# Loading the next eight expert tiles' gates in three parts, in a hybrid attention and PEER kernel on one Trainium2 core

## The chip, the core and the metric

The kernel runs on one core of one Trainium2 chip. The core has a matrix engine (TensorE, PE in the profile, with its weight loads as PEld), a vector engine (VectorE, DVE), a scalar engine (ScalarE, ACT), a general engine (GpSimd, POOL) and an engine that here only starts transfers (SyncE, SP). Each works through its own queue in order and waits for the others by semaphores. Data come from device memory into the on-chip memory of 128 partitions through 16 DMA engines that all queues share. The metric is the device time of one execution in microseconds (us). A change is judged by the median of several executions against that of the kernel before.

## The reference, cut to what matters

One layer over 512 tokens of width 1024. First a gated part and an attention part are added to the input; then comes the part that this change touches, a product-key mixture of 16384 single-row experts (PEER):

```python
def block(xb):                     # tokens in blocks
    q = (xb @ w_query).reshape(PEER_TOKEN_BLOCK, PEER_HEADS, 2, PEER_HALF)
    sc = jnp.einsum('thpd,hpkd->thpk', q, sub_keys)
    s_top, i_top = lax.top_k(sc, PEER_TOPK)
    cand = s_top[:, :, 0, :, None] + s_top[:, :, 1, None, :]
    ...
    best, pos = lax.top_k(cand, PEER_TOPK)
    eidx = jnp.take_along_axis(cand_idx, pos, axis=-1)
    g = jax.nn.softmax(best, axis=-1)
    u = jnp.take(expert_u, eidx, axis=0)
    h = jax.nn.gelu(jnp.einsum('thkd,td->thk', u, xb))
    vv = jnp.take(expert_v, eidx, axis=0)
    return jnp.einsum('thk,thkd->td', (g * h).astype(xb.dtype), vv)
```

Each token picks 8 x 16 experts, weighs them by a softmax, and sums the rows of `expert_v` with the gate times the gelu of a dot product with the row of `expert_u`.

## The kernel before, in words

The 512 tokens are four tiles of 128. One of them, token tile 0, is computed by gathering: for each of its 128 chosen experts per token a row of `expert_u` and a row of `expert_v` is fetched by an indirect transfer from GpSimd (L863 and L874, 512 KB each), and VectorE forms the dot product (L865) and the weighted sum (L876). The other three, 384 tokens, are computed densely: all 16384 experts are multiplied, as 128 expert tiles of 128, and a gate matrix with mostly zeros selects. For 64 of these tokens the first product is spared too, so that the first product has 320 columns (NDU) and the second 384 (NDT).

A weight tile of 512 KB comes through SP into `raw` (L122, three buffers), ScalarE rounds it into `hi` (L124, five buffers), and VectorE, in some places GpSimd, takes the rest into `lo` (L125, five buffers). Products are made of three matmuls each, hi by hi, lo by hi and hi by lo (L140 to L142 for the first product, L932, L933 and L936 for the second).

Before the dense loop the gates of all tiles are made with one-hot matrices (L751) and stored by ScalarE's queue (L757) in `gd`, a tensor in device memory with one block for each eight expert tiles (GB = 8): 128 partitions of 24 groups (NG) of 16 tokens, each group with 8 tiles times 16 tokens in float32. That is 12 KB per partition and 1536 KB per block; there are 16 blocks.

The dense loop (L942) has 64 chunks of two expert tiles (BC = 2). In chunk c, `second_product` takes the two tiles of `expert_v` (`rows_of_v`, L760), multiplies the activations of the chunk by the gates (L910, which reads groups 0 to 19 of the block's tile `gc`), rounds them into `wh` (L911) and `wl` (L912), copies the gates of the 64 spared tokens into the rest of both (L921 and L922, groups 20 to 23), and runs 36 matmuls. Then, while chunks are left that have no first product yet (the first product runs 23 chunks ahead, AHEAD), the first products of chunk c + 23 follow, 48 matmuls with two tiles of `expert_u`. Both stand under a higher priority (PRIO). Behind them come, in chunks 0, 6, 12 and 18, the routing of a quarter of token tile 0 (`route_gathered`, whose scores `sc` are loaded at L847), and in each chunk a share of the gathers.

A block of gates serves four chunks. `gc` has two buffers. Block 0 is loaded by GpSimd in chunk 0, block 1 by SP in chunk 1, tied behind the last weight load so far (`tc.issue_after` puts an instruction behind another in its engine's queue), and block q + 1 by SP in chunk 4q, for q from 1 to 14, in the middle of `second_product`. Its buffer comes free when chunk 4q - 1 has read the block before last (L922).

The order on TensorE is as written (`tc.manual_schedule`). On the other engines a planner sets it when the kernel is built: it takes instructions by priority, which is program order but for the raised pieces, among those whose inputs and buffers are ready by its own estimate of times. The semaphores follow from the data. The names of the lines that matter are L122, L124 and L125 (weight tiles), L897 (the gate load), L910, L921 and L922 (its readers), L863, L865, L874 and L876 (the gathers) and L847 (the scores).

Of the kernel before, what the change touches and what calls it, by code (L numbers as in the profile page):

```python
# [8 lines left out]
F32 = mybir.dt.float32  # L9
# [10 lines left out]
P = 128  # L20
# [30 lines left out]
NB = 128  # L51
BC = 2
# [24 lines left out]
GB = 8  # L77
TC = 8
TG = 16
NG = NDT // TG  # L80
# [7 lines left out]
def hybrid_block(tc, x, ln1, w_in, gng, wsT, bsb, qkg, bias, w_out, ln2, wq, skT, uT, ud, vd, out):  # L88
    nc = tc.nc
    ctx = ExitStack()  # L90
    with ctx:
# [22 lines left out]
        loads = []  # L114
# [150 lines left out]
        with tc.tile_pool(name="preb", bufs=1) as preb:  # L265
# [124 lines left out]
            with tc.manual_schedule(engines={mybir.EngineType.PE}):  # L390
                for i in range(len(steps) + LAG + 3):
# [6 lines left out]
                    if 0 <= i - LAG < len(steps):  # L398
                        t, hs = steps[i - LAG]
                        for h in hs:  # L400
                            transposed(t, h)
                    if 0 <= i - LAG - 1 < len(steps):
                        t, hs = steps[i - LAG - 1]
# [288 lines left out]
        gd = dram.tile([NB // GB, P, NG, GB * TG], F32, name="gd")  # L692
# [67 lines left out]
        def rows_of_v(c):  # L760

            return [load_split(vd.rearrange("(a b) d -> a b d", b=NB)[:, c * BC + b, :]) for b in range(BC)]
# [16 lines left out]
        with tc.manual_schedule(engines=engines):  # L779
# [4 lines left out]
            for n in range(steps + LEAD):  # L784
                t, c = divmod(n, per)
# [50 lines left out]
        ep = ctx.enter_context(tc.tile_pool(name="ep", bufs=1))  # L836
# [55 lines left out]
        accs = [[acx[:, 0:512], acx[:, 512:]]] + [[pa() for _ in range(2)] for _ in range(ND - 1)]  # L892
        gcs = {}

        def load_gates(q, eng):
            gcs[q] = ep.tile([P, NG, GB, TG], F32, name="gc", tag="gc", bufs=2)
            eng.dma_start(gcs[q].rearrange("p n b t -> p (n b t)"), gd[q].rearrange("p n f -> p (n f)"))  # L897

        def second_product(c):
            w = weights.pop(c) if c in weights else rows_of_v(c)  # L900
            if c == 0:
                load_gates(0, nc.gpsimd)
            gc = gcs[c * BC // GB]
            act = acts.pop(c)
            wh = ep.tile([P, BC, NDT], F32R, name="wh", tag="wh", bufs=2)
            wl = ep.tile([P, BC, NDT], F32R, name="wl", tag="wl", bufs=2)
            for b in range(BC):
                bb = (c * BC + b) % GB
                av = act[:, b, :].rearrange("p (n t) -> p n t", t=TG)
                nc.vector.tensor_tensor(av, av, gc[:, 0:NDU // TG, bb, :], op=ALU.mult)  # L910
            nc.scalar.activation(wh[:, :, 0:NDU], act, AF.Copy)  # L911
            mark = nc.vector.tensor_tensor(wl[:, :, 0:NDU], act, wh[:, :, 0:NDU].bitcast(F32), op=ALU.subtract)  # L912
            if c == 1:
                with tc.issue_after(loads[-1]):
                    load_gates(1, nc.sync)
            elif c * BC % GB == 0 and 0 < c * BC < NB - GB:
                load_gates(c * BC // GB + 1, nc.sync)
            b0 = (c * BC) % GB
            gu = gc[:, NDU // TG:, b0:b0 + BC, :]
            hu, lu = (w_[:, :, NDU:].rearrange("p b (n t) -> p n b t", t=TG) for w_ in (wh, wl))  # L920
            nc.scalar.activation(hu, gu, AF.Copy)  # L921
            nc.vector.tensor_tensor(lu, gu, hu.bitcast(F32), op=ALU.subtract)  # L922
            order = [(b, t) for b in range(BC) for t in range(ND)]
            if c == NCHK - 1:
                order.sort(key=lambda bt: bt[1])
            for b, t in order:
                first = c == 0 and b == 0
                last = c == NCHK - 1 and b == BC - 1
                tok = slice(t * P, (t + 1) * P)
                for half in range(2):  # L930
                    ds_ = slice(half * 512, (half + 1) * 512)
                    nc.tensor.matmul(accs[t][half], wh[:, b, tok], w[b][0][:, ds_], start=first, stop=False)  # L932
                    nc.tensor.matmul(accs[t][half], wh[:, b, tok], w[b][1][:, ds_], start=False, stop=False)  # L933
                for half in range(2):
                    ds_ = slice(half * 512, (half + 1) * 512)
                    nc.tensor.matmul(accs[t][half], wl[:, b, tok], w[b][0][:, ds_], start=False, stop=last)  # L936
            return mark
# [3 lines left out]
        with tc.manual_schedule(engines={mybir.EngineType.PE}):  # L941
            for c in range(NCHK):  # L942
                with tc.high_priority(offset=PRIO):
                    mark = second_product(c)
                    if c + AHEAD < NCHK:
                        for _ in first_products((c + AHEAD) * BC, BC):
                            pass
                if c % ROUTE == 0 and c < PARTS * ROUTE:
                    route_gathered(c // ROUTE)
                passed = c + 1 + min(c + 1, NCHK - AHEAD)  # L950
                with tc.issue_after(mark.ins if hasattr(mark, "ins") else mark):
                    gather_some(min(total, total * max(0, passed - DELAY) // (weight - SLACK - DELAY))
                                - (total - len(gathers)))
            gather_some(len(gathers))
# [53 lines left out]
```

## Time and profile before

| what | value |
|---|---|
| median of 3 runs | 1493.92 us |
| lowest and highest | 1490.16 and 1494.91 us |
| the profiled execution's own time | 1489.67 us |
| its span, first to last instruction | 1487.9 us |
| mean granted TensorE clock | 0.984 |
| expert loop in it | from about 641 us to the end |
| gate loads | 1 by GpSimd at 630.5, 15 by SP from 648.5 to 1409.4 us |
| moved by DMA | 396.78 MB, 267 GB/s over the span |

The profile is of one execution; its times count from the first instruction. Busy time of an engine leaves out its waits. In a row of the timeline stand the start, the time, engine and line, the operation, the output and inputs by the program's names with their shapes, how many such instructions in a row, and in square brackets the time for which the engine stood idle before and what ended that wait. SPq and POOLq are the queues in which transfers are started. Matmuls are pipelined, so that each shows a longer time than its distance to the next. The granted clock is the share of full speed at which TensorE was allowed to run.

### The profile page before, as it was taken

The page shows a single profiled execution, that of the slowest core. Times are in us where ns is not written, and L with a number is a line of the kernel's source. Part 1 is how long each engine was busy: PE and PEld are TensorE (multiplying, and loading weights), DVE is VectorE, ACT ScalarE, POOL GpSimd, SP SyncE. Part 2 cuts the span into 40 slices and gives each one's busy share as a digit, 9 for nine tenths or more (in the row PEclk, how much of TensorE's full clock was granted, in tenths as well). Part 3 has the DMA queues.
Part 4 walks back from the last instruction along what each step waited for, and adds up shares of the span by engine and source line. Part 5 has one row for each costly group of instructions (what it writes and reads, how often), then busy time and mean ns, then how long its engine had stood idle before and what let it go on. Part 6 is the DMA issues. An engine that isn't in the chain of part 4 may idle for free.

```text
span 1487.9 us, 21702 instructions
## 1 busy us (share of the span) xinstructions
PE 1403.9 (94%) x7804; PEld 1235.9 (83%) x7804; DVE 1158.7 (78%) x2345; ACT 641.9 (43%) x1108; POOL 690.4 (46%) x470
## 2 busy tenths in 40 slices
PE   7999999998878888999989899999999999999998
PEld 6886678987777888888978799888999989888886
DVE  5437554699996968688988789898888888688883
ACT  5447534332335677743434333343343333333331
POOL 0000016687867966504435555464555554344530
PEclk9999999998998999999999999999999999999999
DMA  5352226576765976878878799999999999879992
GB/s 184 114 184 71 86 102 186 184 260 230 282 230 165 324 219 198 240 256 310 300 284 331 290 376 330 350 355 349 389 350 357 368 341 367 305 285 341 333 356 85
DMA packets 161420, 396.78 MB, mean 267 GB/s; under 512 B 12304, under 2 KB 74528, under 8 KB 159264
## 3 DMA queue, kind: packets, MB, share of 16 engines
q1 hardware_dynamic: 62992, 197.42, 37.4%
q0 software_dynamic: 47488, 171.50, 31.1%
q10 hardware_dynamic: 50832, 26.48, 6.3%
q8 instruction: 61, 1.00, 0.3%
q14 instruction: 47, 0.39, 0.1%
HBM read 363.86 MB, written 31.46 MB: 266 GB/s over the span
## 4 chain that ended last, share of the span: by engine, by line
PE 51%; DVE 19%; DMA 13%; issue 7%; POOL 5%; ACT 4%; ACTq 0%; SPq 0%; DVEq 0%; POOLq 0%
PE pu L140 6%; PE pu L142 6%; PE pu L141 6%; PE pa L932 5%; PE pa L933 5%; PE pa L936 5%; DMA row<-in_vd,eint 5%; DVE rowe L489 3%; PE px L933 3%; PE px L932 3%; PE px L936 3%; DMA row<-in_ud,eint 3%; PE pa L140 2%; PE pa L141 2%; PE pa L142 2%
## 5 line engine op out<-in xcount | busy, mean ns | idle before, releaser
L124 ACT ACTIVATE hi<-raw 128x1024 fp32r<-128x1024 f32 x300 | 317.3, 1058 | 511.0 <-DMA raw<-in_vd 185.2
L125 DVE TENSOR_TENSOR lo<-raw,hi 128x1024 fp32r<-128x1024 f32 x251 | 309.5, 1234 | 109.5 <-ACT hi L124 108.4
L874 POOL DMA_INDIRECT row<-in_vd,eint x128 | 196.9, 1538 | 196.8 <-DVE acc L876 165.2
L863 POOL DMA_INDIRECT row<-in_ud,eint x128 | 184.6, 1442 | 190.3 <-DVE row L865 149.1
L140 PE MATMUL pu<-xch,hi 128*128 128x320 f32 x816 | 257.7, 316 | 3.5 <-ACT act L546 2.9
L142 PE MATMUL pu<-xch,lo 128*128 128x320 f32 x816 | 252.6, 310 | 2.6 <-POOL lo L125 2.0
L141 PE MATMUL pu<-xcl,hi 128*128 128x320 f32 x816 | 252.5, 309 | 0.0
L932 PE MATMUL pa<-hi,wh 128*128 128x512 f32 x512 | 200.9, 392 | 0.0
L933 PE MATMUL pa<-lo,wh 128*128 128x512 f32 x512 | 200.5, 392 | 0.0
L876 DVE SCALAR_TENSOR_TENSOR acc<-row,hw,acc 128x1024 f32<-128x1024 f32 x128 | 165.1, 1290 | 40.4 <-DMA row<-in_vd,eint 40.1
L865 DVE SCALAR_TENSOR_TENSOR row<-row,xb 128x1024 f32<-128x1024 f32 x128 | 156.3, 1223 | 28.9 <-DMA row<-in_ud,eint 28.5
L140 PEld LDWEIGHTS pu<-xch,hi 128*128 128x128 f32 x816 | 154.7, 190 | 7.2 <-ACT act L546 5.0
L936 PE MATMUL pa<-hi,wl 128*128 128x512 f32 x512 | 158.1, 390 | 0.0
L142 PEld LDWEIGHTS pu<-xch,lo 128*128 128x128 f32 x816 | 154.3, 189 | 3.8 <-POOL lo L125 2.2
L141 PEld LDWEIGHTS pu<-xcl,hi 128*128 128x128 f32 x816 | 154.6, 189 | 1.5
L125 POOL TENSOR_TENSOR lo<-raw,hi 128x1024 fp32r<-128x1024 f32 x49 | 117.8, 2416 | 77.2 <-ACT hi L124 73.3
L751 PE MATMUL pa<-bm,am 128*128 128x128 f32 x768 | 99.0, 283 | 19.9 <-POOL bm L730 13.7
L751 PEld LDWEIGHTS pa<-bm,am 128*128 128x128 f32 x768 | 93.3, 196 | 25.1 <-POOL bm L730 22.6
L932 PEld LDWEIGHTS pa<-hi,wh 128*128 128x128 f32 x512 | 96.8, 189 | 20.6
L933 PEld LDWEIGHTS pa<-lo,wh 128*128 128x128 f32 x512 | 96.8, 189 | 20.5
L936 PEld LDWEIGHTS pa<-hi,wl 128*128 128x128 f32 x512 | 96.6, 189 | 20.6
L933 PE MATMUL px<-lo,wh 128*128 128x512 f32 x256 | 101.0, 395 | 7.2 <-DVE lo L125 7.2
(215 smaller groups left out, 2635.1 us busy)
## 6 DMA issues: line engine op xcount, KB each, us to landing
raw<-in_uT SPq DMA_DIRECT2D x128, 512.0 KB, 5.8
raw<-in_vd SPq DMA_DIRECT2D x128, 512.0 KB, 5.6
gd<-gst ACTq DMA_DIRECT2D x24, 1024.0 KB, 6.2
gc<-gd SPq DMA_DIRECT2D x15, 1536.0 KB, 9.7
raw<-in_w_in SPq DMA_DIRECT2D x20, 512.0 KB, 4.7
raw<-in_wq SPq DMA_DIRECT2D x16, 512.0 KB, 3.8
raw<-in_w_out SPq DMA_DIRECT2D x8, 512.0 KB, 4.2
bt<-in_bias SPq DMA_DIRECT2D x8, 256.0 KB, 7.4
```

The source lines that it names most:

```text
L124: nc.scalar.activation(hi, raw, AF.Copy)
L125: eng.tensor_tensor(lo, raw, hi.bitcast(F32), op=ALU.subtract)
L140: nc.tensor.matmul(ps, lh[0], rh[0], start=first, stop=False)
L141: nc.tensor.matmul(ps, lh[0], rh[1], start=False, stop=False)
L142: nc.tensor.matmul(ps, lh[1], rh[0], start=False, stop=last)
L751: nc.tensor.matmul(ps[:, i * P:(i + 1) * P], am[:, 4 * q + i, :], bm[:, 4 * q + i, :], start=True, stop=True)
L863: nc.gpsimd.indirect_dma_start(out=row, out_offset=None, in_=ud, in_offset=bass.IndirectOffsetOnAxis(ap=eint[:, j:j + 1], axis=0))
L874: nc.gpsimd.indirect_dma_start(out=row, out_offset=None, in_=vd, in_offset=bass.IndirectOffsetOnAxis(ap=eint[:, j:j + 1], axis=0))
L876: nc.vector.scalar_tensor_tensor(acc0, row, hw[:, j:j + 1], acc0, op0=ALU.mult, op1=ALU.add)
L932: nc.tensor.matmul(accs[t][half], wh[:, b, tok], w[b][0][:, ds_], start=first, stop=False)
L933: nc.tensor.matmul(accs[t][half], wh[:, b, tok], w[b][1][:, ds_], start=False, stop=False)
L936: nc.tensor.matmul(accs[t][half], wl[:, b, tok], w[b][0][:, ds_], start=False, stop=last)
```

## The change

Blocks 1 to 15 of the gates come in three transfers of 8 groups each (512 KB, 4 KB per partition), where they came in one of 24 groups. For block q + 1, part 0 stands in chunk 4q, part 1 in chunk 4q + 1 and part 2 in chunk 4q + 2, always behind L912. For block 1, parts 0 and 1 stand in chunk 1, tied behind the last weight load so far as the whole load was, and part 2 in chunk 2, without such a tie. All three parts write into the same `gc` tile, which is taken with part 0. Block 0 is still loaded whole by GpSimd. L910 and L921 read what they read before.

```diff
-        def load_gates(q, eng):
-            gcs[q] = ep.tile([P, NG, GB, TG], F32, name="gc", tag="gc", bufs=2)
-            eng.dma_start(gcs[q].rearrange("p n b t -> p (n b t)"), gd[q].rearrange("p n f -> p (n f)"))
+        def load_gates(q, eng, part=0, parts=1):
+
+            if part == 0:
+                gcs[q] = ep.tile([P, NG, GB, TG], F32, name="gc", tag="gc", bufs=2)
+            ns = slice(part * NG // parts, (part + 1) * NG // parts)
+            eng.dma_start(gcs[q][:, ns].rearrange("p n b t -> p (n b t)"),
+                          gd[q, :, ns].rearrange("p n f -> p (n f)"))
...
-            if c == 1:
-                with tc.issue_after(loads[-1]):
-                    load_gates(1, nc.sync)
-            elif c * BC % GB == 0 and 0 < c * BC < NB - GB:
-                load_gates(c * BC // GB + 1, nc.sync)
+            q, part = divmod(c, GB // BC)
+            parts = GB // BC - 1
+            if q + 1 < NB // GB:
+                if c == 0:
+                    pass
+                elif c == 1:
+                    with tc.issue_after(loads[-1]):
+                        load_gates(1, nc.sync, 0, parts)
+                        load_gates(1, nc.sync, 1, parts)
+                elif part < parts:
+                    load_gates(q + 1, nc.sync, part, parts)
```

## The prediction

> **What bounds the kernel now.** I read the page's header and engine shares first, then the stretches of the expert loop, then TensorE's waits in them.
>
> ```profile
> span 1487.9 us, 21702 instructions
> PE 1403.9 (94%) x7804; PEld 1235.9 (83%) x7804; DVE 1158.7 (78%) x2345; ACT 641.9 (43%) x1108; POOL 690.4 (46%) x470
> ```
>
> ```profile
> 670.00:870.00 200.00, 189.60 (x1014) 168.11 (x1014) 174.17 (x384) 76.44 (x112) 97.95 (x65) 0.98 0.84 310
> 870.00:1295.00 425.00, 424.45 (x2338) 383.26 (x2337) 364.85 (x465) 162.48 (x232) 221.53 (x151) 1.00 0.95 352
> 1295.00:1470.00 175.00, 175.00 (x773) 144.87 (x773) 137.36 (x178) 63.00 (x86) 67.03 (x43) 1.00 0.82 301
> ```
>
> The columns are stretch, length, then busy time and count of PE, PEld, DVE, ACT and POOL, then the granted clock, the DMA share and GB/s. From 870 to 1470 TensorE is busy for 599.45 of 600 us at a clock of 1.00: whatever the gates do there, nothing can be won. Only between 670 and 870 is there something to win: 200 - 189.60 = 10.4 us of idle PE, and a clock of 0.98, worth 0.02 x 200 = 4 us. So 14 us is the ceiling of any gain in the loop, 0.9% of the whole. The three longest holes, in the timeline of PE:
>
> ```profile
> 754.09 0.42 PE L140 MATMUL pu<-xch,hi 128*128 128x320 f32 x1 [1.68 <-ACT act L546]
> 768.65 0.59 PE L933 MATMUL px<-lo,wh 128*128 128x512 f32 x1 [2.88 <-DVE lo L125]
> 849.28 0.50 PE L933 MATMUL px<-lo,wh 128*128 128x512 f32 x1 [3.74 <-DVE lo L125]
> ```
>
> Two of them wait for VectorE's `lo`, the low half of a split weight tile. What VectorE and GpSimd did ahead of the one at 768.65:
>
> ```profile
> 755.91 1.68 POOL L874 DMA_INDIRECT row<-in_vd,eint  x1 [9.59 <-DVE acc L876]
> 765.77 1.28 DVE L876 SCALAR_TENSOR_TENSOR acc<-row,hw,acc 128x1024 f32<-128x1024 f32 x1 [4.38 <-DMA row<-in_vd,eint]
> 766.98 0.48 DVE L910 TENSOR_TENSOR act<-act,gc 128x320 f32<-128x320 f32 x1
> 767.38 1.22 DVE L125 TENSOR_TENSOR lo<-raw,hi 128x1024 fp32r<-128x1024 f32 x1
> ```
>
> ```profile
> 754.47 0.33 SPq L897 DMA_DIRECT2D gc<-gd  x1
> ```
>
> The `lo` that PE needs stands in VectorE's queue behind a gathered row that landed late (issued at 755.91, used at 765.77), while the gates' 1.5 MB, issued at 754.47, was in flight. The hole at 849.28 stands behind a gathered row too, but no gate load flies then: the last one before it was issued at 817.26, 30 us earlier.
>
> ```profile
> 817.26 0.52 SPq L897 DMA_DIRECT2D gc<-gd  x1
> 846.86 1.23 DVE L865 SCALAR_TENSOR_TENSOR row<-row,xb 128x1024 f32<-128x1024 f32 x1 [4.38 <-DMA row<-in_ud,eint]
> ```
>
> So the gate load is party to one hole out of the three.
>
> What the gate load costs its neighbours is read from the DMA issues of two short windows at full load, 1004.4 to 1010 with a gate load and 1022 to 1036 without one (the last number is the median from issue to landing):
>
> ```profile
> gc<-gd SPq DMA_DIRECT2D x1, 1536.0 KB, 11.0
> raw<-in_vd SPq DMA_DIRECT2D x1, 512.0 KB, 11.2
> row<-in_vd,eint POOLq DMA_INDIRECT x1, 11.0
> row<-in_ud,eint POOLq DMA_INDIRECT x1, 11.2
> ```
>
> ```profile
> raw<-in_vd SPq DMA_DIRECT2D x1, 512.0 KB, 6.1
> row<-in_vd,eint POOLq DMA_INDIRECT x3, 7.8
> row<-in_ud,eint POOLq DMA_INDIRECT x3, 7.5
> ```
>
> A weight tile queued behind the gates lands 11.2 - 6.1 = 5.1 us later, a gathered row 11.0 - 7.8 = 3.2 or 11.2 - 7.5 = 3.7 us later.
>
> **The change part by part.** It removes fifteen transfers of 1536 KB from SP's queue and puts 45 of 512 KB there. The bytes, the buffers and the readers are the same; tile 0 is still loaded whole by GpSimd.
>
> *Where the parts will stand.* In program order parts 1 and 2 come one and two chunks behind part 0, but only for tile 1 are parts 0 and 1 tied to a weight load. SP's order is the planner's, and the trace shows what the planner does with a load whose buffer is free:
>
> ```profile
> 658.36 0.33 SPq L122 DMA_DIRECT2D raw<-in_vd  x1
> 658.74 0.43 SPq L847 DMA_DIRECT2D sc<-s0d  x1
> ```
>
> ```profile
> 1015.80 3.30 DVE L910 TENSOR_TENSOR act<-act,gc 128x320 f32<-128x320 f32 x8
> ```
>
> The first `sc` load that SP issues is written behind chunk 6 of the loop. Chunks start near 641 and take some 15 us (425 us of full PE in 2338 matmuls, 84 to a chunk, is 15.3), so its place is near 733; it went out at 658.74. The L910 products show the same on VectorE: all eight of a gate tile, for four chunks, in one run as soon as it lands. One event, the last use of the buffer's earlier tile, frees the place of all three parts at once. So I expect the three issues back to back, or with a weight load between, not chunks apart: mostly the change will not do what its words say.
>
> *SP's time.*
>
> ```profile
> L897 SPq DMA_DIRECT2D gc<-gd x15: 326/327/1065, 648.5 to 1409.4; - x15
> L897 POOLq EVENT_SEMAPHORE  x8: 43/43/43, 619.8 to 630.0; - x8
> ```
>
> ```profile
> SPq L122 <- DVE lo L125: 523.6, 165, 9.6
> ```
>
> Thirty more issues of 0.33 us are 9.9 us of SP, which waits 523.6 us for weight buffers to come free: 0 on the path. Without that cover the load behind the parts goes out 0.66 us late. L910 reads groups 0 to 19 of 24, hence all three parts: two more waits per tile, 30 at the 43 ns of the nearest row, are 1.3 us of VectorE. VectorE is idle for 27.1 us between 641.3 and 870:
>
> ```profile
> 641.30:870.00 228.70, 201.57 (x482) 0.98 0.81 297
> ```
>
> So 0 again, and 1.3 us if the cover is gone.
>
> *The DMA engines' time.*
>
> ```profile
> DMA packets 161420, 396.78 MB, mean 267 GB/s; under 512 B 12304, under 2 KB 74528, under 8 KB 159264
> q1 hardware_dynamic: 62992, 197.42, 37.4%
> q0 software_dynamic: 47488, 171.50, 31.1%
> ```
>
> 161420 - 159264 = 2156 packets are of 8 KB or more, and 16 gate loads x 128 partitions are 2048: gates move in packets of 12 KB, where the change makes 4 KB ones. On q0 a packet takes 0.311 x 16 x 1487.9 / 47488 = 0.156 us for 3.6 KB, so by bytes 0.18 us for 4 KB and 0.53 us for 12 KB: the total stays. What may change is the turn of a gathered row beside the gates: 512 KB are 8 packets on each of 16 engines. If queues take turns by packets, a row sits out 8 x 0.53 = 4.2 us of gates, and 8 x 0.18 = 1.4 us after the change: 2.8 us sooner, the size of the 3.2 us measured above. If turns go by bytes, or the gates' neighbour is a weight tile in the same queue, nothing changes. Ends: 0 and -2.88 us, the hole at 768.65, plus its clock:
>
> ```profile
> 764.00:774.00 10.00, 7.12 (x24) 5.38 (x23) 8.23 (x14) 2.44 (x3) 0.95 (x1) 0.83 0.81 308
> ```
>
> 0.17 x 10 = 1.7 us, so -4.6 at most. I take half, -2.3 us, since both readings are open. The Trainium skill (DMA: Bandwidth & Descriptors, Queues, rings and completion order) says that each DMA engine serves the queue rows in turn, a packet at a time. By that rule the gather's 2.8 us are won, and the term would be near -4.6 instead of -2.3.
>
> *The loop's start.* Part 2 of tile 1 stands in chunk 2 and is tied to nothing, and its buffer is free from the start. Like the `sc` load it can go out as soon as the gates are stored, beside tile 0's load that PE waits for:
>
> ```profile
> 638.90 0.89 DVE L910 TENSOR_TENSOR act<-act,gc 128x320 f32<-128x320 f32 x2 [4.47 <-DMA gc<-gd]
> 630.00:640.00 10.00, 7.62 (x52) 7.36 (x51) 3.24 (x6) 2.36 (x5) 2.39 (x4) 1.00 0.98 394
> ```
>
> At a share of 0.98, 0.52 MB at 394 GB/s are 1.3 us. Ends: 0 (it hides behind weight tiles, which have time) and +1.3; I take +0.5, since it adds to another queue than tile 0's.
>
> *The other engines' order.* The planner orders the work again with other landing times. No row prices that. The ends are -14 us (all of 670 to 870 repaired) and +14 (its holes twice); I take 0.
>
> Sum: 1489.67 (the profiled execution: the span of 1487.9 and 1.77 around it) - 2.3 + 0.5 = 1487.9. The median of the three runs, 1493.92, lies 4.25 above the profiled one; on that footing the time is **1492 us**.
>
> **The rivals.** *Spread out after all, faster.* If a weight load becomes ready between the parts, each keeps one 512 KB part ahead of it and not three. Two thirds of the 5.1 us delay go, 3.4 us, and gathers lose their long neighbour. The hole at 768.65 goes whole with its clock, 4.6 us: 1489. For it: weight loads follow the gates within 2.3 us, so a little planner's time between the parts lets one in:
>
> ```profile
> 1004.48 0.33 SPq L897 DMA_DIRECT2D gc<-gd  x1
> 1006.81 0.33 SPq L122 DMA_DIRECT2D raw<-in_vd  x1
> ```
>
> Against it: one release for all three parts, and an SP that mostly waits.
>
> *VectorE waits for three landings, slower.* VectorE takes its queue in order, and L910 is put there early, by the planner's idea of when gates land. Where that idea is too early it already stands idle:
>
> ```profile
> 1350.95 2.10 DVE L910 TENSOR_TENSOR act<-act,gc 128x320 f32<-128x320 f32 x5 [3.47 <-DMA gc<-gd]
> ```
>
> After 1295 PE does not feel it. If the parts look quicker to the planner than one transfer, L910 moves forward everywhere, and `lo` stands behind it. Four gate loads go out on SP before 870, the first at 648.5 and the last at 817.3. VectorE's slack there is 27.1 us over 15 chunks, 1.8 us a chunk, so it decides once a wait exceeds 1.8: 3.47 - 1.8 = 1.7 us of PE for each of four tiles, 6.8, and clock in the ratio 4 to 10.4, 2.6: +9.4, so 1503. Against it: before 870 no wait of 3 us for gates delays PE now.
> The Trainium skill (DMA: Bandwidth & Descriptors, Anatomy of one DMA) gives each transfer, on GpSimd's path, some 2 us of fixed cost. Three in series would then cost 4 us more than one, an estimate, and this rival would hold; the rows above speak against a series: gates issued at 1004.48 landed 11.0 us later, the weight tile issued at 1006.81 11.2 us later, so 512 KB more came only 2.5 us behind, under full load.
>
> **How the numbers follow.** The forecast gets 0.45, with an own range of 1487 to 1497; spread out 0.28; the VectorE wait 0.27. A measurement of this kernel tells about 0.3% (4.5 us) from no change. Of the forecast 0.11 falls to faster, 0.30 to same, 0.04 to slower; of the spread, which lies just at the bound, 0.18 to faster and 0.10 to same; of the wait 0.07 to same and 0.20 to slower. Faster 0.29, same 0.47, slower 0.24. The range takes in the faster rival with 5 us of planner's luck below it and stops just short of the slower one: 1484 to 1502.
>
> **What would show it.** SP's timeline: three L897 issues within a microsecond or two (mine) or a chunk apart (the spread). Packets: near 165,260 in all (15 x 256 more), with some 240 of 8 KB or more. L897 at about 631 in SP's queue shows the start's term, and a PE gap before 641 its price. PE idle between 670 and 870 under 8 us says the gather term is real; over 16 us with L910 waiting for gates, the slower rival. I am wrong if PE gets holes behind 870, which would mean that the planner's new order costs more than any row here.

## The result, and the profile after

The changed kernel takes 1511.38 us (median of 4 runs, 1507.32 to 1520.42), where the kernel before took 1494.41 (4 runs). The ratio is 1.0116, with a 95% interval from 1.0076 to 1.0156: 17 us slower, where 1492 us, no change, was the forecast and 1502 the end of the range.

The profiled execution of the changed kernel (1507.32 us), its header and engine shares:

```profile
span 1505.5 us, 21751 instructions
PE 1413.2 (94%) x7804; PEld 1242.6 (83%) x7804; DVE 1164.1 (77%) x2345; ACT 642.6 (43%) x1108; POOL 688.9 (46%) x470
```

The first matmul of the second products, in the timeline of PE, after:

```profile
653.84 0.80 PE L942 MATMUL px<-hi,wh 128*128 128x512 f32 x1 [5.00 <-ACT wh L915]
```

and before:

```profile
641.28 0.50 PE L932 MATMUL px<-hi,wh 128*128 128x512 f32 x1 [3.66 <-ACT wh L911]
```

So of the 17.6 us between the two spans 12.6 lie ahead of the loop's start, in code that the change does not touch but for 5.00 - 3.66 = 1.3 us, and 5.0 behind it. These proportions are those of two single executions; the experiments below show others.

The stretches of the loop, after, moved back by 13 us so that they answer to those of before (the same columns):

```profile
683.00:883.00 200.00, 193.35 (x1045) 172.16 (x1044) 179.39 (x391) 77.74 (x113) 99.34 (x67) 0.99 0.86 317
883.00:1308.00 425.00, 419.68 (x2307) 377.67 (x2307) 359.11 (x460) 161.61 (x229) 222.36 (x150) 1.00 0.93 348
1308.00:1483.00 175.00, 171.40 (x750) 141.45 (x749) 137.20 (x177) 61.85 (x84) 64.29 (x43) 0.99 0.82 303
```

PE's idle time went from 10.4 to 6.7 us in the first stretch, from 0.6 to 5.3 in the second and from 0 to 3.6 in the third. In this execution what was won early was lost where PE had been full; the clean pair below has the loss without the early win.

SP's queue, after, at the loop's start and at the last block:

```profile
640.96 0.33 SPq L900 DMA_DIRECT2D gc<-gd  x1
641.34 0.42 SPq L122 DMA_DIRECT2D raw<-in_uT  x1
...
1423.67 0.86 SPq L900 DMA_DIRECT2D gc<-gd  x2
1427.11 0.33 SPq L122 DMA_DIRECT2D raw<-in_vd  x1
1427.49 0.65 SPq L900 DMA_DIRECT2D gc<-gd  x1
1430.17 14.27 SPq L122 DMA_DIRECT2D raw<-in_vd  x3
```

The parts do not go out a chunk apart, but two at once, one weight load, and the third. The untied part of block 1 stands ahead of weight loads at 640.96. The packets of the changed kernel:

```profile
DMA packets 165741, 396.79 MB, mean 264 GB/s; under 512 B 12784, under 2 KB 75008, under 8 KB 165504
```

165741 - 165504 = 237 packets of 8 KB or more are left of 2156. What the hole of 3.6 us in the third stretch waited for, from the timelines of ScalarE, VectorE and PE after, and the granted clock in the window behind it:

```profile
1435.57 1.06 ACT L124 ACTIVATE hi<-raw 128x1024 fp32r<-128x1024 f32 x1 [4.97 <-DMA raw<-in_vd]
```

```profile
1438.17 0.49 DVE L914 TENSOR_TENSOR act<-act,gc 128x320 f32<-128x320 f32 x1 [3.52 <-DMA gc<-gd]
1438.58 1.22 DVE L125 TENSOR_TENSOR lo<-raw,hi 128x1024 fp32r<-128x1024 f32 x1
1439.72 2.09 DVE L914 TENSOR_TENSOR act<-act,gc 128x320 f32<-128x320 f32 x5
1441.73 0.81 DVE L916 TENSOR_TENSOR wl<-act,wh 128x640 fp32r<-128x640 f32 x1
```

```profile
1442.60 1.22 PE L946 MATMUL px<-hi,wl 128*128 128x512 f32 x2 [3.60 <-DVE wl L916]
```

```profile
1442.60:1445.40 2.80, 2.80 (x7) 2.22 (x8) 2.80 (x5) 1.26 (x2) 0.00 (x0) 0.50 0.06 19
```

VectorE stands at the first product with the new gates; behind it in its queue are the `lo` and the `wl` of the work that PE needs now. The weight tile is late as well. After the hole PE runs 2.8 us at a clock of 0.50, which costs another 1.4 us. The same block before:

```profile
1409.43 0.42 SPq L897 DMA_DIRECT2D gc<-gd  x1
```

```profile
1419.16 2.10 DVE L910 TENSOR_TENSOR act<-act,gc 128x320 f32<-128x320 f32 x5 [3.02 <-DMA gc<-gd]
```

There VectorE had the gates 1419.16 - 1409.43 = 9.7 us after their issue, now 1438.17 - 1423.67 = 14.5 us.

### The profile page after: what moved, and what is told of

Same layout as the page of the kernel before. It is cut to its first block, busy times and chain, and to the rows that moved or that the text cites. A ratio compares the mean times of both kernels' runs of the same rounds, so it can differ in the third digit from the quotient of the medians.

```text
span 1505.5 us, 21751 instructions
## 1 busy us (share of the span) xinstructions
PE 1413.2 (94%) x7804; PEld 1242.6 (83%) x7804; DVE 1164.1 (77%) x2345; ACT 642.6 (43%) x1108; POOL 688.9 (46%) x470
## 2 busy tenths in 40 slices
DMA packets 165741, 396.79 MB, mean 264 GB/s; under 512 B 12784, under 2 KB 75008, under 8 KB 165504
## 4 chain that ended last, share of the span: by engine, by line
PE 58%; DVE 15%; DMA 10%; issue 7%; POOL 5%; ACT 4%; ACTq 0%; SPq 0%; DVEq 0%; POOLq 0%
PE pu L140 7%; PE pu L141 7%; PE pu L142 7%; PE pa L942 6%; PE pa L943 6%; PE pa L946 6%; DMA row<-in_vd,eint 4%; DVE rowe L489 3%; PE px L946 3%; PE px L942 3%; PE px L943 3%; PE pa L140 2%; PE pa L141 2%; PE pa L142 2%; DMA row<-in_ud,eint 2%
## 5 line engine op out<-in xcount | busy, mean ns | idle before, releaser
L124 ACT ACTIVATE hi<-raw 128x1024 fp32r<-128x1024 f32 x300 | 317.1, 1058 | 540.3 <-DMA raw<-in_vd 209.8
L125 DVE TENSOR_TENSOR lo<-raw,hi 128x1024 fp32r<-128x1024 f32 x251 | 309.1, 1232 | 104.4 <-ACT hi L124 103.2
L874 POOL DMA_INDIRECT row<-in_vd,eint x128 | 204.2, 1595 | 224.5 <-DVE acc L876 194.1
L863 POOL DMA_INDIRECT row<-in_ud,eint x128 | 175.8, 1374 | 167.4 <-DVE row L865 126.9
L876 DVE SCALAR_TENSOR_TENSOR acc<-row,hw,acc 128x1024 f32<-128x1024 f32 x128 | 165.8, 1295 | 42.3 <-DMA row<-in_vd,eint 41.9
L125 POOL TENSOR_TENSOR lo<-raw,hi 128x1024 fp32r<-128x1024 f32 x49 | 118.6, 2432 | 84.8 <-ACT hi L124 78.5
```

The lines of the kernel that those rows point to most:

```text
L124: nc.scalar.activation(hi, raw, AF.Copy)
L125: eng.tensor_tensor(lo, raw, hi.bitcast(F32), op=ALU.subtract)
L863: nc.gpsimd.indirect_dma_start(out=row, out_offset=None, in_=ud, in_offset=bass.IndirectOffsetOnAxis(ap=eint[:, j:j + 1], axis=0))
L874: nc.gpsimd.indirect_dma_start(out=row, out_offset=None, in_=vd, in_offset=bass.IndirectOffsetOnAxis(ap=eint[:, j:j + 1], axis=0))
L876: nc.vector.scalar_tensor_tensor(acc0, row, hw[:, j:j + 1], acc0, op0=ALU.mult, op1=ALU.add)
```

## The experiments

The recorded expectations weigh theories by name. TURNS is that gates in small packets lose their share of the DMA engines to the gathered rows, so that they, and the weight tiles behind them in SP's queue, land later. Its rivals were that the order or the number of the transfers costs, and that the loss is one of the time ahead of the loop. LAYOUT, a rival that comes in later, is that the order of the gates in device memory costs, not the size of their packets. All ratios are to the kernel before on the same chip, with 95% intervals.

**The two kernels again.** No edit.

> The changed kernel once more, unaltered. Three theories of the extra 17 us of the changed kernel (1511.38 against 1494.41 us). LOOP: the change costs 5 to 8 us itself, 1 to 2 at the loop's start (PE waits 5.0 us there against 3.7) and 4 to 6 in the loop (VectorE waits for three gate landings); then this run is 5 to 9 us above the kernel before. LUCK: the 11.2 us that were lost before 620 us, in instructions that are the same and in the same order, are chance: VectorE's L601 was caught behind GpSimd's L125 three times in eight where the kernel before was caught twice, at about 7 us each; then this run's profile has another number of caught L601 and the time before the loop moves by 7 us a piece. FIXED: the time before the loop is longer in every run of the changed kernel; then the profile again shows the loop's first second-product matmul near 654 us and the time is again 12 to 20 us above.

> The kernel before as its own rival, unaltered: a null. All theories: ratio 1.000. It shows how wide a ratio of two equal kernels comes out, and how many L601 are caught in another profile of the same program. LUCK expects a time before the loop that differs from the first profile's 641 us by 0 or about 7 or 14 us; FIXED expects 641 within 2 us.

The changed kernel: 1519.22 us, ratio 1.0107 [1.0081, 1.0133]. The kernel before: 1498.70 us, 0.9974 [0.9951, 0.9997]. The loss repeats. The second interval just leaves out 1 for two copies of one program, so differences near 0.3% are not told apart here. The kernel before also showed that its time ahead of the loop varies by itself; PE in its second profile:

```profile
651.54 0.80 PE L932 MATMUL px<-hi,wh 128*128 128x512 f32 x1 [3.67 <-ACT wh L911]
```

10.3 us later than in the first, with every instruction the same. The 11 us that the changed kernel's profile lost there need no change to explain them.

**Without the three parts' places.** Three parts, issued together where the whole load stood:

```diff
...
+            if c == 1:
+                with tc.issue_after(loads[-1]):
+                    for part in range(3):
+                        load_gates(1, nc.sync, part, 3)
+            elif c * BC % GB == 0 and 0 < c * BC < NB - GB:
+                for part in range(3):
+                    load_gates(c * BC // GB + 1, nc.sync, part, 3)
```

> The split alone: all three parts in the one place where the whole load stood (chunk 4q, and tied in chunk 1). If the split itself costs (three landings, L910 put earlier by the planner), the loop's loss of 4 to 6 us is here too, without the start's: 4 to 6 us above the kernel before. If moving the parts to later chunks costs, this one is within 2 us of the kernel before.

1514.71 us, 1.0089 [1.0064, 1.0114]: not told apart from the changed kernel, and some 13 us where 4 to 6 were expected. So the loss does not need the later places. The edit also ties part 2 of block 1, so that it changes two things at once; what the places do with that tie in both kernels is taken up below.

**Truly spread.** Every part is tied behind the last weight load so far:

```diff
                 elif part < parts:
-                    load_gates(q + 1, nc.sync, part, parts)
+                    with tc.issue_after(loads[-1]):
+                        load_gates(q + 1, nc.sync, part, parts)
```

> The change as its words say it: every part tied behind the weight load of its own chunk, so that in SP's order a chunk's four weight loads lie between the parts in the stage with both products. TURNS: the amount of 4 KB packets is the same but never more than 512 KB stand in a row, so a weight tile has one part ahead of it: PE idles less in the last 23 chunks than in the other split kernels (under 4 us against 3.6 to 10.6) and the time is 0 to 6 us above the kernel before. ORDER: VectorE waits for the third landing as long as before or longer, since it comes a chunk or two later: 5 to 13 us above.

SP's queue in it, and PE's largest wait from 640 us on:

```profile
1216.89 0.43 SPq L900 DMA_DIRECT2D gc<-gd  x1
...
1233.49 0.43 SPq L900 DMA_DIRECT2D gc<-gd  x1
...
1247.55 0.43 SPq L900 DMA_DIRECT2D gc<-gd  x1
```

```profile
PE px L947 <- DVE wl L916: 14.0, 5, 4.5
```

Now the parts of this block stand some 15 us apart, and the kernel is slower still: 1523.01 us, 1.0143 [1.0101, 1.0184]. The prediction's faster rival falls. So do both expectations, 0 to 6 us by TURNS and 5 to 13 by ORDER, where some 21 were lost. TURNS alone does not give this number: VectorE's products need all three parts, and the third is issued 1247.55 - 1216.89 = 30.7 us after the first.

**Small packets alone.** The number and the places of the transfers are those of the kernel before, and in the traces every engine has the same instructions in the same order. Only the layout of `gd` differs, so that a load's pieces are 4 KB, those of block 0's load by GpSimd too; the stores that fill `gd` ahead of the loop go to other addresses:

```diff
-        gd = dram.tile([NB // GB, P, NG, GB * TG], F32, name="gd")
+        gd = dram.tile([NB // GB, 3, P, NG // 3, GB * TG], F32, name="gd")
...
-            eng.dma_start(gcs[q].rearrange("p n b t -> p (n b t)"), gd[q].rearrange("p n f -> p (n f)"))
+            eng.dma_start(gcs[q].rearrange("p (h n) b t -> p h (n b t)", h=3),
+                          gd[q].rearrange("h p n f -> p h (n f)"))
```

> The kernel before, with one change of layout: a block of gates lies in device memory as three pieces of 8 groups, so that the one transfer of 1536 KB moves in packets of 4 KB where they were 12 KB (block 0's transfer and the stores of the gates too). Number of transfers and their place in SP's queue are those of the kernel before. TURNS: queues take turns by packets, gates in 4 KB packets get half of the DMA engines beside gathers where 12 KB ones got three quarters, so gates and the weight tiles behind them land some 4 us later; in the last 23 chunks, where PE needs two weight tiles per 8 us, PE then idles 4 to 10 us (0.0 in the kernel before, 8.3 and 10.6 in two of the split kernels) and the time is 5 to 13 us above. ORDER: the split kernels lose because their parts stand among weight loads and the third waits for a weight buffer; then this kernel has the order of the kernel before and is within 2 us of it, PE idle in the last 23 chunks under 1 us. COUNT (a fixed cost per transfer): as ORDER.

1523.57 us, 1.0134 [1.0096, 1.0173]: as much as the changed kernel loses and more than the 5 to 13 us that TURNS expected, without the change's parts, its waits or another order. The same with 2 and with 6 parts in `gd`:

> The same in two parts per block, packets of 6 KB, still one transfer at the old place. TURNS: between 12 KB (1.000) and 4 KB (1.0134), nearer to the latter since a row's packet of 4 KB is two thirds of it: 1.003 to 1.010. LAYOUT: 1.010 to 1.017 as at 4 KB, since the order is as different and the pieces still start 6 KB apart in the tile.

> The kernel before, every gate block in one transfer at its old place, but stored in six parts per block, so that it comes in packets of 2 KB. TURNS: a queue's share goes by the size of its packets, so half of 4 KB loses more than 4 KB did (1.0134): 1.018 to 1.035, most of it behind 1295, and gate products that wait longer than at 4 KB. LAYOUT (what costs is the other order of the gates in device memory or the longer list of pieces, not their size beside a row's 4 KB): 1.010 to 1.017 as at 4 KB.

| packets of the gates | time, us | ratio | median landing of a load, 660 to 1480 us |
|---|---|---|---|
| 12 KB (the kernel before) | | 1 | 9.8 us |
| 6 KB | 1510.79 | 1.0071 [1.0042, 1.0099] | 11.3 us |
| 4 KB | 1523.57 | 1.0134 [1.0096, 1.0173] | not in the trace |
| 2 KB | 1530.15 | 1.0219 [1.0183, 1.0256] | 13.1 us |

LAYOUT, which wanted the same loss at all sizes, falls: the time follows the size of the packets. What VectorE waited for the gates from 640 us on, in the waits of the kernels with 6, 4 and 2 KB (total, times, longest), where the kernel before has 13.9 us, or 18.4 with its wait for block 0, which there falls just ahead of 640:

```profile
DVE act L911 <- DMA gc<-gd: 33.9, 14, 5.2
```

```profile
DVE act L911 <- DMA gc<-gd: 57.4, 15, 7.7
```

```profile
DVE act L911 <- DMA gc<-gd: 75.1, 14, 8.4
```

That small packets are dear in themselves does not explain it. SP's queue at 4 KB:

```profile
q1 hardware_dynamic: 66832, 197.42, 36.8%
```

Its packets take 0.368 x 1524.3 = 560.9 us of the 16 engines' time, where before they took 0.374 x 1487.9 = 556.5: 4.4 us more in all, 0.3 for each of 16 loads. So the gates wait between their packets, and the packet records in the traces show for what. Between 660 and 1480 us SP's queue and GpSimd's are the only two that take more than 0.3% of the engines' time, and GpSimd's then carries the gathered rows. From the first packet of a load by SP to its last it is 6.4 us at 12 KB, 7.6 at 6 KB and 9.5 at 2 KB (means), and in that time GpSimd's queue moves 0.64, 1.03 and 1.49 MB; the load's own packets take 3.9, 3.9 and 4.4 us of each engine. It is the gathered rows that go ahead.

**What is luck, taken out.** Ahead of the loop VectorE's L601 takes 0.46 us, and sometimes 7. The timelines of GpSimd and VectorE after show one:

```profile
294.92 7.09 POOL L125 TENSOR_TENSOR lo<-raw,hi 128x1024 fp32r<-128x1024 f32 x3
```

```profile
294.60 7.75 DVE L601 TENSOR_TENSOR pa<-bpos,bits 128x288 uint32<-128x288 uint32 x1
```

It ends when three of GpSimd's L125 have ended. So one of its two inputs was moved from SBUF to PSUM, in the kernel before:

```diff
+            where = bpos.rearrange("p t k -> p (t k)")
+            if mask.shape[-1] > 6 * n * TOPK:
+                moved = mask[:, 6 * n * TOPK:7 * n * TOPK]
+                mask = mask[:, 0:6 * n * TOPK]
+                nc.scalar.copy(moved, where)
+                where = moved
...
-                                    bpos.rearrange("p t k -> p (t k)")[:, None, :]
+                                    where[:, None, :]
```

> The kernel before; in the eight rounds of routing for the dense tiles the positions are first copied by ScalarE into the PSUM bank of the mask, so that VectorE's L601 has one input in PSUM and one in on-chip memory, not two in on-chip memory. LUCK by the two engines' common access: no L601 is caught behind GpSimd's L125 any more (2 and 3 of 8 at 7 us in two profiles of the kernel before); the loop then starts 7 to 15 us earlier than the 641 to 652 us seen, or less where PE did not wait for it, and the runs lie closer together. If L601 is caught for another reason (its output in PSUM, its type), it is caught as often as before and the time is the same within 4 us.

1487.72 us, 0.9927 [0.9901, 0.9954], faster than both kernels; a second measurement beside the next kernel:

> The kernel before with L601 reading from PSUM, once more, so that the changed kernel with the same edit has its own base on the same chip: 0.990 to 0.995 by both theories.

1489.83 us, 0.9942 [0.9920, 0.9964]. L601 in it, under its new line number (shortest, median, longest in ns):

```profile
L607 DVE TENSOR_TENSOR pa<-pa,bits x8: 451/458/461, 277.9 to 444.0; 128x288 uint32<-128x288 uint32 x8
```

None of the eight is caught. The loop starts at 643.36 and 639.74 us in the two profiles of this kernel, no earlier than the 641.28 of the kernel before, where two of eight were caught, but earlier than its 651.54, where three were. The edit also moves other instructions ahead of the loop, so that the gain is not shown to be L601's alone. The Trainium skill (SBUF — State Buffer, SBUF: two separate sides) says that a VectorE operation with two SBUF inputs and a GpSimd operation that reads SBUF lock each other out for a whole instruction. The row agrees and goes further: the wait lasted over three GpSimd instructions in a row, 7 us. Then the changed kernel got the same edit:

> The changed kernel with the L601 of the kernel before it in this text: the positions are copied once by ScalarE into PSUM and VectorE's L601 reads them there, so that it isn't caught behind GpSimd's L125 any more. TURNS (gates in 4 KB packets lose their share of the DMA engines to the gathered rows, all of it in the expert loop): the price of the change stays when the luck ahead of the loop is taken out of both: 1.008 to 1.014 times the kernel before with the same L601, so 1.001 to 1.007 against the kernel before. LUCK ALONE (what the change costs is that L601 is caught more often in it): the price is gone, 0.990 to 0.995 against the kernel before, as the kernel before with this L601.

1505.55 us, 1.0044 [1.0023, 1.0066]. Against its own base that is 1.0044 / 0.9942 = 1.0103, about 1.007 to 1.013 with the two intervals' half widths added in square: the price of the change stays when the luck is out of both. This pair, the clean pair from here on, starts its loops together; PE with the old gates:

```profile
639.74 0.50 PE L938 MATMUL px<-hi,wh 128*128 128x512 f32 x1 [4.09 <-ACT wh L917]
```

and with the three parts:

```profile
640.00 0.79 PE L948 MATMUL px<-hi,wh 128*128 128x512 f32 x1 [5.01 <-ACT wh L921]
```

So nearly all of the 1501.7 - 1488.3 = 13.4 us between their spans is lost in the loop. Its stretches with the old gates:

```profile
670.00:870.00 200.00, 190.36 (x1018) 168.74 (x1017) 175.28 (x378) 76.70 (x113) 94.11 (x66) 0.98 0.85 314
870.00:1295.00 425.00, 424.11 (x2335) 382.52 (x2335) 361.31 (x464) 162.71 (x231) 228.18 (x152) 1.00 0.95 352
1295.00:1470.00 175.00, 173.25 (x765) 143.14 (x764) 136.49 (x178) 61.41 (x84) 67.21 (x42) 1.00 0.82 298
```

and with the three parts:

```profile
670.00:870.00 200.00, 189.95 (x1021) 168.37 (x1020) 175.97 (x382) 77.23 (x113) 96.77 (x66) 0.99 0.86 314
870.00:1295.00 425.00, 419.96 (x2289) 375.95 (x2288) 352.71 (x453) 156.24 (x223) 216.38 (x149) 1.00 0.92 342
1295.00:1470.00 175.00, 168.59 (x748) 139.26 (x747) 141.68 (x183) 63.41 (x88) 69.67 (x46) 0.99 0.86 320
```

PE idles 0.4, 4.2 and 4.7 us more in the three stretches: nothing is won in the first, and both others lose. The rest of the 13.4 us is not in these idle times; how much the clock behind the holes bears is not worked out. Who waited for transfers from 640 us on, old gates:

```profile
ACT hi L124 <- DMA raw<-in_vd: 203.7, 75, 7.2
ACT hi L124 <- DMA raw<-in_uT: 91.9, 42, 7.2
DVE acc L882 <- DMA row<-in_vd,eint: 43.8, 30, 4.4
DVE row L871 <- DMA row<-in_ud,eint: 35.3, 25, 4.0
DVE act L916 <- DMA gc<-gd: 13.3, 5, 4.7
```

and three parts:

```profile
ACT hi L124 <- DMA raw<-in_vd: 252.6, 95, 7.2
ACT hi L124 <- DMA raw<-in_uT: 143.5, 56, 9.4
DVE acc L882 <- DMA row<-in_vd,eint: 44.3, 31, 4.6
DVE act L920 <- DMA gc<-gd: 32.4, 9, 5.2
DVE row L871 <- DMA row<-in_ud,eint: 19.6, 22, 2.1
```

The gathered rows of `expert_u` win 15.7 us of VectorE's wait, those of `expert_v` win nothing, and the gates lose 19.1. ScalarE's waits for weight tiles grow by 48.9 + 51.6 = 100.5 us, but its waits for PE (L124 and the rounding into `wh`) shrink by 74 us: mostly the tile now comes last where PE did. The median weight tile lands as before (`expert_v` 5.6 and 5.8 us after its issue, `expert_u` 6.6 and 6.5), and so does the median row (7.5 and 7.5; 7.7 and 7.9), all between 660 and 1480 us.

**The untied part, and the late blocks.** First only part 2 of block 1 was tied like its neighbours; then blocks 12 to 15 were loaded whole besides:

```diff
+                elif c == 2:
+                    with tc.issue_after(loads[-1]):
+                        load_gates(1, nc.sync, 2, parts)
+                elif q + 1 >= 12:
+                    if part == 0:
+                        load_gates(q + 1, nc.sync)
```

> The changed kernel with part 2 of block 1 tied behind the last weight load, as parts 0 and 1 are. In SP's order it then no longer stands ahead of the weight loads of the loop's start. LOOP: PE's wait at the loop's start goes back from 5.0 to about 3.7 us, the time falls 1 to 3 us below the changed kernel, and the rest of the loop's loss (4 to 6 us) stays. If the stray load is the main cost, the time falls to within 3 us of the kernel before.

> The changed kernel with its stray part tied, and the last four blocks (12 to 15) loaded whole in chunk 4q as before. If all of the loop's loss arises in the last 23 chunks, PE idles under 1 us there, the stretch from the last first-product matmul to the last matmul is 188 us as in the kernel before (193 to 204 in the split kernels), and the time is within 3 us of the kernel before, or 1 to 4 us below it, since the stage with both products took 650 us in two split kernels and 653 before. If the loss has another place, it stays 3 us or more above.

1505.40 us, 1.0022 [1.0002, 1.0042], and 1503.66 us, 1.0030 [1.0003, 1.0056]. PE's wait at the loop's start is 4.05 us with the tie. The tie takes back four fifths of the loss in the same comparison (1.0107), far more than the 5.00 - 4.05 = 0.95 us of this wait. It also changes SP's order up to 743 us, ScalarE's to 798 and VectorE's to 812, behind which the orders are the same as without it. The stretches with the tie, moved by 3 us:

```profile
673.00:873.00 200.00, 196.36 (x1072) 175.50 (x1071) 182.35 (x391) 78.96 (x114) 96.44 (x68) 1.00 0.89 329
873.00:1298.00 425.00, 419.95 (x2303) 377.52 (x2303) 355.51 (x456) 160.57 (x229) 216.53 (x148) 1.00 0.93 346
1298.00:1473.00 175.00, 170.97 (x744) 140.28 (x743) 137.04 (x178) 61.43 (x84) 65.59 (x43) 0.99 0.82 300
```

PE idles 3.6 us in the first stretch, where the changed kernel had 6.7 and the kernel before 10.4, and behind it 5.1 and 4.0, as the changed kernel did (5.3 and 3.6). So in this profile the tie gains in the first chunks, where it changes the order, and the loss behind them stays. This profile is of the fastest of its runs (1495.37), and where the median's whole gain lies is open. The tie by itself does not save: the kernels with three parts at one place and with the parts truly spread have part 2 of block 1 tied too and cost 0.9 and 1.4%. With that tie in all three, the places of the other parts, and the order that the planner makes of them, move the time by over 1%.

Block 14 reaches VectorE 1396.04 - 1383.47 = 12.6 us after its issue as a whole load, and 1393.11 - 1376.99 = 16.1 us after the first part's issue with the tie alone; yet VectorE waits 3.87 and 3.94 us for it, and the time is not told apart. As the tie alone leaves only 0.2%, there was little for this run to bring back.

**Where the loss lies.** The table has, from PE's timelines, the time from the first matmul of the second products to the first of the last 23 chunks, which have second products alone, and from there to the last matmul:

| kernel | both products, us | last 23 chunks, us |
|---|---|---|
| before, two profiles | 653.3, 653.4 | 187.5, 188.4 |
| changed, two profiles | 653.5, 655.6 | 192.8, 200.1 |
| old gates, L601 from PSUM, two profiles (the first is the clean pair's) | 653.1, 649.2 | 189.6, 187.5 |
| clean pair, three parts | 660.1 | 196.1 |
| three parts at one place | 651.0 | 203.4 |
| truly spread | 652.8 | 210.5 |
| with the tie | 649.9 | 194.1 |
| the tie, late blocks whole | 649.0 | 192.4 |
| whole loads, 6, 4, 2 KB | 656.1, 658.6, 667.5 | 195.0, 204.4, 206.2 |

Every kernel with smaller packets is some 3 us or more behind every one with 12 KB packets in the last 23 chunks. Ahead of them the kernels differ in both directions, partly because single profiles do: two of one kernel are 4 us apart there (653.1 and 649.2), and 7 in the last chunks (192.8 and 200.1).

## Why the prediction was wrong

*Where the parts stand, SP's time, the packets.* Right: issues within microseconds, no SP cost that shows, 237 packets of 8 KB or more where some 240 were expected.

*The loop's start.* Right: part 2 goes out ahead of weight loads and costs 5.00 - 3.66 = 1.3 us, the upper end; 5.01 - 4.09 = 0.9 in the pair with PSUM.

*The DMA engines' time.* This is the step that failed. It took turns by packets as open, and priced only the side of the queue that wins: a gathered row 2.8 us sooner, 0 to -4.6, taken as -2.3. The turns have another side, for what a row gains per turn the gates and what stands behind them in SP's queue lose. The prediction had a row that shows what such a delay is (a weight tile behind the gates lands 5.1 us later) and read "or the gates' neighbour is a weight tile in the same queue, nothing changes". In the place of -2.3 us, 4 KB packets with the order held cost 1.3%, some 20 us, and the clean pair some +13. The win did not show either: idle PE between 670 and 870 is 9.6 and 10.1 us in the clean pair, though the one profile after has under 8, the sign that was named for it. The Trainium skill's rule that it quoted (DMA: Bandwidth & Descriptors, Queues, rings and completion order), turns by the packet, agrees with the series over 12, 6, 4 and 2 KB in its direction. It is not shown that a turn is one packet of the profile, as the prediction took it: the same section gives a packet some 9 to 17 descriptors, and beside a row's 4 KB pieces single turns would give a load 3, 1.5 and 0.5 times the rows' bytes at 12, 6 and 2 KB, where 1.57 MB against 0.64, 1.03 and 1.49 are 2.5, 1.5 and 1.1. The term that was drawn from the rule had the wrong sign.

*"Whatever the gates do there, nothing can be won" (870 to 1470), "After 1295 PE does not feel it".* The first is true, and hid that much can be lost there. The second is not true of the changed kernel: in the last block a wait of 3.02 us for gates made no hole, and one of 3.52, with the gates 4.8 us later after their issue, stands ahead of one of 3.60. The length of the wait alone does not decide, for the 3.47 us that the prediction shows at 1350.95 made no hole before. How much the late weight tile beside it bears, these rows do not tell.

*The rivals.* The slower one had the mechanism: `lo` and `wl` behind the products with the gates. It placed it before 870, where idle PE is 9.6 and 10.1 us in the clean pair, and at 1503 it was too cheap. It put it down to a planner that moves L910 forward. From block 4 on, the first product of each block stands in VectorE's order at the same place as before or up to four places later, so it is the landings that come later. The faster one, parts spread out, was measured at 1.0143.

*The planner's order.* Taken as 0 with ends of -14 and +14 for want of a row. The runs with the same 4 KB packets and different orders lie between 1.0022 and 1.0143, 18 us apart, so the second thing that the sum had at nothing is as large as the loss itself. How the changed kernel's loss divides between its packets and its order is open; that the packets alone are enough is shown.

## What to carry over

Where queues share the DMA engines, the size of the contiguous piece per partition is a load's weight in that contest: before cutting a load, ask what shrinks, its bytes in flight or its packets, and price the loser of the turns as well as the winner. A full engine in the profile says that nothing is to be won there, not that it has slack; look for waits one step upstream (here some 3 us of VectorE at L910) that it covers. And where a program's copies differ by 10 us ahead of the changed code, find what is caught there and take it out of both sides. An edit that moves a planner's order has a price of its own, which only a run with the order held tells apart.

## What the runs showed of the hardware

With the same bytes, order and count of transfers, gates in pieces of 6, 4 and 2 KB instead of 12 made the whole kernel 0.7, 1.3 and 2.2% slower; while one load ran, the other busy queue moved 1.03 MB at 6 KB and 1.49 at 2 KB instead of 0.64. A VectorE operation of 0.46 us with two SBUF inputs stood 7.75 us beside three GpSimd operations in a row, and none of eight did so with one input in PSUM; the kernel with that edit, which also moves other instructions, was 0.6 to 0.7% faster. After a hole of 3.6 us PE had a clock of 0.50 for 2.8 us, so that a hole costs more than its length; the Trainium skill (TensorE: Matmul & The Clock Gate, What's actually happening) has an idle TensorE at half rate until it has been busy for some 3.4 us, which is near what the row shows.
